# The mixer's first norm factor made on GpSimd instead of TensorE, ScalarE and VectorE

## Chip, core and metric

The kernel runs on one core of one Trainium2 chip. The metric is the device time of one execution in microseconds. Five engines work side by side, each through its own queue in order: TensorE (PE, with its weight loads as PEld), VectorE (DVE), ScalarE (ACT), GpSimd (POOL) and SyncE (SP), which here only issues DMAs. They wait for one another on semaphores.

## The reference

One step of a decoder trunk for 512 new prompt tokens and 8 decode tokens, 1024 features, one layer: a half-step SwiGLU FFN, a hybrid mixer, another half-step FFN, a final norm. What matters is how the mixer's input is normed and where that goes:

```python
def _rms_norm(x, g):
    y = xf * lax.rsqrt(jnp.mean(xf * xf, axis=-1, keepdims=True) + EPS)
    return (y * g.astype(jnp.float32)).astype(x.dtype)
...
def _hybrid_mixer(h, ...):
    proj = h @ w_in
    u_pool, z, xbc, dt_raw = jnp.split(proj, ...)
    ...
    dt = jax.nn.softplus(dt_raw + dt_bias)
...
h = h + 0.5 * _swiglu(_rms_norm(h, ffn1_norm[l]), ...)
m, p, c, s = _hybrid_mixer(_rms_norm(h, mix_norm[l]), ...)
```

The causal convolution over x, B and C, a pooling mixer, the scan over chunks of 128 tokens and a gated norm follow inside the mixer.

## The kernel before

Features lie on the 128 partitions (8 blocks of 128), the 520 tokens along the free axis, in two halves of 260 (HALVES). Every weight and activation is split into a high and a low part; a product is three matmuls (high by high, high by low, low by high). ScalarE makes the high part of a weight (whi, thi), VectorE the low part (wlo, tlo) from the raw tile, which SyncE's queue loads.

The norm is applied late. While the first FFN ends, prep makes xh_mx and xl_mx (the features times the norm's weight, not yet times the factor) and adds the squares of the 8 feature blocks into acc_mx. The factor is one number per token, 1 / sqrt(mean + epsilon), wanted on every partition: the tile r_mx, 128 x 520. rstds makes it half by half: a matmul of acc_mx with a matrix of ones sums over the partitions and leaves the sum on all of them (psr_mx, in PSUM), ScalarE takes the root with scale 1/1024 and epsilon as bias, VectorE the reciprocal. in_proj's products (inbc, inx, inp, inz) are made from xh_mx and xl_mx without the factor, and each is multiplied by r_mx when VectorE copies it from PSUM (evac; dv for the step sizes).

The mixer starts with the small product for the step sizes (dt, two halves, in two PSUM banks), then the factor, then dv, then the plan CONV_PLAN, "b0 b1 d0 b2 b3 x0 x1 v0 d1 x2 x3 d2 ...". A b or x is one block of in_proj (inbc00 and inbc01 are the halves of block b0) with its convolution: U is the copy scaled by the factor, A takes one ScalarE pass and three VectorE passes over it, then a Silu. d0 is token_dt: TensorE brings dv into token order (psdv), and a chain of some 20 small steps on VectorE and ScalarE makes the step sizes (dt_v, dt_e, dt_s, dt_q, tok) and dta. d1 is token_acs: TensorE multiplies dta with a triangle (psacs). The mixer has 8 PSUM banks, handed out in turn, so a product that isn't copied out holds its bank.

The order within each engine's queue isn't the order of the code: a list scheduler places the instructions when the program is built, by the dependences, the order of the code as priority, and its own idea of durations. A few are tied by hand (issue_after, keep_in_program_order). GpSimd does small things here: it clears and fills the edges of U, copies states out, and later adds the pooling windows. Its queue holds no DMA between the first FFN's end and the output projection.

Of the kernel before, what the change touches and what calls it, by code (L numbers as in the profile page):

```python
# [4 lines left out]

# [4 lines left out]

F32 = mybir.dt.float32
F32R = mybir.dt.float32r
AF = mybir.ActivationFunctionType
ALU = mybir.AluOpType
# [3 lines left out]
P = 128  # L18
D = 1024
SEQ = 512  # L20
NS = 8
NT = SEQ + NS
HB = NT // 2
HALVES = (slice(0, HB), slice(HB, NT))
# [3 lines left out]
EPS = 1e-6  # L28
# [40 lines left out]
def tile_trunk_step(ctx: ExitStack, tc: tile.TileContext, ins: dict, outs: dict):  # L69
# [733 lines left out]

    ps[0] = tc.alloc_tile_pool(name="ppm", bufs=8, space=PSUM, reuse_waits="tile")
    mixer(tc, ins, outs, dict(locals()))
    f2["xg"].release()
    xa[0].release()
# [90 lines left out]
def mixer(tc, ins, outs, e):  # L898
    nc = tc.nc
    cst, act, wp, tmp, dr, pool = (e[x] for x in ("cst", "act", "wp", "tmp", "dr", "pool"))  # L900
    ones, queued, squared = e["ones"], e["queued"], tuple(e["added"])
    bank, load_unit, mm3, mm_low_last, ws, v, rstd, rstds, vec, h, nx2, raw_tile, open_f2, fin, fill = (
        e[x] for x in ("bank", "load_unit", "mm3", "mm_low_last", "ws", "v", "rstd", "rstds", "vec", "h", "nx2", "raw_tile",
                       "open_f2", "fin", "fill"))
    xh, xl, _, r = nx2[0]
    xa = e["xa"][0]
    mp = pool("mx", "right")
# [45 lines left out]
    for b, hs in enumerate(HALVES):  # L953
        for k in range(KD):
# [2 lines left out]
            nc.tensor.matmul(dtb[b][:48, :HB], w48[:, k], xh[:, k, hs], start=k == 0, stop=k == KD - 1)  # L957
            if not k:
                nc.tensor.matmul(dtb[b][:NH, :HB], w48[:, k, :NH], xl[:, k, hs], start=False, stop=False)
    rstds(nx2[0], "mx")  # L960
    dv = mp.tile([48, NT], F32, tag="h0", bufs=4, name="dv")
    for b, hs in enumerate(HALVES):
        nc.vector.tensor_tensor(out=dv[:, hs], in0=dtb[b][:48, :HB], in1=r[:48, hs], op=ALU.mult)
# [522 lines left out]
```

## Time and profile before

| | |
|---|---|
| time of the kernel, median of 3 runs | 954.13 us (953.25 to 955.27) |
| the profiled execution's own time, first to last instruction (span) | 951.9 us |
| between the span and the median of the runs | 2.2 us |
| TensorE busy | 942.5 us (99%) |
| VectorE busy | 852.7 us (90%) |
| ScalarE busy | 635.7 us (67%) |
| GpSimd busy | 148.3 us (16%) |

The profile is of one execution. A row of the timeline has the start in the span, the duration, the engine, the line of the kernel, the operation with its output and inputs, and in square brackets the idle time before it with what ended it. A group by line or tile gives least, median and longest duration in ns. Starts of successive rows overlap a little, so what an instruction costs its engine is read from start to start.

### The profile page before, as it was taken

How to read it: one execution, taken by the hardware profiler on the slowest of the kernel's cores; microseconds unless marked ns; L12 is line 12 of the kernel's file. 1: busy time of each engine (PE TensorE's matmuls, PEld its weight loads, DVE VectorE, ACT ScalarE, POOL GpSimd, SP SyncE). 2: the span in 40 equal slices, each digit the busy share in tenths (PEclk: the TensorE clock that was granted, in tenths of full speed). 3: DMA queues.
4: the chain of work that ended last, by engine and by line, in shares of the span. 5: the costliest groups of instructions: out<-in, count | busy, mean ns of one | idle time of the engine just before them, and what ended most of it. 6: DMA issues, size and time to landing. Idle time of an engine off the chain costs nothing.

```text
span 951.9 us, 19681 instructions
## 1 busy us (share of the span) xinstructions
PE 942.5 (99%) x7674; PEld 925.9 (97%) x7674; DVE 852.7 (90%) x1462; ACT 635.7 (67%) x1179; POOL 148.3 (16%) x230
## 2 busy tenths in 40 slices
PE   9999999999999999999999999999999999999996
PEld 8999999999999999999999999999999999999996
DVE  6899899998988688789998998999999999999886
ACT  7777756677566455485668735777776676766774
POOL 0011100100100000046251100111112101122120
PEclk9999999999999999999999999999999999999998
DMA  7666554455553343354264453556666655776552
GB/s 205 187 166 150 143 151 135 115 140 156 134 155 95 86 134 122 92 180 138 91 184 133 141 114 115 138 122 160 163 173 176 163 146 144 171 194 185 145 180 91
DMA packets 53995, 138.35 MB, mean 145 GB/s; under 512 B 7750, under 2 KB 15878, under 8 KB 53902
## 3 DMA queue, kind: packets, MB, share of 16 engines
q1 hardware_dynamic: 39918, 104.19, 34.2%
q0 software_dynamic: 13712, 32.78, 18.7%
q8 instruction: 60, 0.98, 0.4%
q14 instruction: 33, 0.27, 0.1%
q10 hardware_dynamic: 272, 0.13, 0.0%
HBM read 129.74 MB, written 7.34 MB: 144 GB/s over the span
## 4 chain that ended last, share of the span: by engine, by line
PE 44%; DVE 2%; issue 1%; POOL 1%; DMA 1%; ACT 1%; DVEq 0%; ACTq 0%; POOLq 0%
PE A L160 8%; PE BE L160 6%; PE wo L160 5%; PE A L165 4%; PE BE L165 3%; PE wo L165 2%; PE P L311 1%; PE dh L155 1%; PE dh L151 1%; PE dh L154 1%; POOL zs L1068 1%; PE inz L151 1%; PE inz L154 1%; PE inz L155 1%; DMA room<-in_state_ssm 1%
## 5 line engine op out<-in xcount | busy, mean ns | idle before, releaser
L504 ACT COPY ac<-A 128x260 f32<-128x260 f32 x85 | 31.6, 372 | 35.4 <-PE A L155 17.3
L433 DVE TENSOR_TENSOR s<-raw 128x1024 f32<-128x1024 f32 x39 | 47.6, 1222 | 4.4 <-DMA raw<-in_w2gu 2.8
L504 ACT COPY ac<-BE 128x260 f32<-128x260 f32 x41 | 15.4, 376 | 33.6 <-PE BE L165 17.7
L151 PE MATMUL inx<-xh_mx,whi_inx 128*128 128x260 f32 x112 | 31.8, 284 | 0.0
L154 PE MATMUL inx<-xl_mx,whi_inx 128*128 128x260 f32 x112 | 31.6, 282 | 0.0
L155 PE MATMUL inx<-xh_mx,wlo_inx 128*128 128x260 f32 x112 | 31.6, 282 | 0.0
L1027 DVE SCALAR_TENSOR_TENSOR A<-U,h,A 128x544 f32<-128x544 f32 x36 | 29.0, 807 | 1.6 <-ACT A L1025 1.2
L311 PE MATMUL P<-x,raw 128*128 128x260 f32 x128 | 28.9, 385 | 0.2 <-DMA raw<-in_w1gu 0.2
L311 PEld LDWEIGHTS P<-x,raw 128*128 128x128 f32 x128 | 24.4, 192 | 4.2 <-DMA raw<-in_w1gu 0.6
L160 PE MATMUL wo<-catg,whi_wo 128*128 128x260 f32 x192 | 27.4, 285 | 0.0
L1193 ACT ACTIVATE so<-br,sxdt 128x128 f32<-128x128 f32 x64 | 22.8, 376 | 5.8 <-DVE room L1195 5.2
L160 PEld LDWEIGHTS wo<-catg,whi_wo 128*128 128x128 f32 x192 | 24.8, 188 | 0.2
L139 ACT CAST thi<-raw 128x1024 fp32r<-128x1024 f32 (+1 forms) x14 | 14.2, 1012 | 15.7 <-PE wo L160 4.8
L1304 DVE TENSOR_TENSOR h<-wo,h 128x260 f32<-128x260 f32 x48 | 19.2, 422 | 5.0 <-PE wo L165 4.7
L252 DVE TENSOR_TENSOR gs<-gq,gs 128x780 fp32r<-128x780 f32 (+1 forms) x28 | 23.3, 831 | 0.0
L151 PE MATMUL inz<-xh_mx,whi_inz 128*128 128x260 f32 x80 | 23.0, 287 | 0.0
L154 PE MATMUL inz<-xl_mx,whi_inz 128*128 128x260 f32 x80 | 22.7, 284 | 0.0
L155 PE MATMUL inz<-xh_mx,wlo_inz 128*128 128x260 f32 x80 | 22.6, 283 | 0.0
L251 ACT CAST gs<-gq 128x780 fp32r<-128x780 f32 (+1 forms) x28 | 20.6, 735 | 1.2 <-DVE gq L555 0.8
L151 PEld LDWEIGHTS inx<-xh_mx,whi_inx 128*128 128x128 f32 x112 | 21.1, 188 | 0.2 <-issue 0.2
L160 PE MATMUL A<-xth_f,qs 128*128 128x260 f32 x84 | 21.2, 283 | 0.0
L160 PE MATMUL A<-xtl_f,qs 128*128 128x260 f32 x84 | 21.2, 284 | 0.0
(3140 smaller groups left out, 4382.9 us busy)
## 6 DMA issues: line engine op xcount, KB each, us to landing
raw<-in_w2gu SPq DMA_DIRECT2D x44, 512.0 KB, 4.4
raw<-in_w1gu SPq DMA_DIRECT2D x41, 512.0 KB, 4.3
raw<-in_w_in SPq DMA_DIRECT2D x24, 512.0 KB, 3.7
raw<-in_w1d SPq DMA_DIRECT2D x16, 512.0 KB, 4.6
raw<-in_w2d SPq DMA_DIRECT2D x16, 512.0 KB, 4.6
raw<-in_w_out SPq DMA_DIRECT2D x12, 512.0 KB, 3.5
ab<-scr_acs SPq DMA_DIRECT2D x8, 512.0 KB, 5.5
h<-in_state_ssm SPq DMA_DIRECT2D x16, 256.0 KB, 3.7
```

The lines of the kernel that those rows point to most:

```text
L151: first = nc.tensor.matmul(ps, whi, xhi, start=start, stop=False, **kw)
L154: nc.tensor.matmul(ps, whi, xlo, start=False, stop=False, **kw)
L155: nc.tensor.matmul(ps, wlo, xhi, start=False, stop=stop, **kw)
L160: mm = nc.tensor.matmul(ps, w, x, start=start, stop=False, **kw)
L165: nc.tensor.matmul(ps, w, xhi[k], start=False, stop=k == len(wlo) - 1, **kw)
L251: cast = nc.scalar.copy(hi, s)
L252: low = nc.vector.tensor_tensor(out=lo, in0=s, in1=hi.bitcast(F32), op=ALU.subtract)
L311: mm = nc.tensor.matmul(self.banks[f, u][b][:, :HB], ws(self.raw[f][:, u], j + 4 * q), xg[:, slot[q]], start=j == q == 0, stop=j == 3 and ...
L433: nc.vector.tensor_tensor(out=s1, in0=diag, in1=up0, op=ALU.add)
L504: self.copied = nc.scalar.copy(keep, out[:, :HB]).ins
L1027: nc.vector.scalar_tensor_tensor(out=A[:, :n], in0=U[:, j : j + n], scalar=w(j), in1=A[:, :n], op0=ALU.mult, op1=ALU.add)
L1193: nc.scalar.activation(out=o[:, q], in_=br, func=AF.Copy, scale=sxdt[:, j, b : b + 1]))
```

## The change

The call of rstds for the mixer is replaced. GpSimd sums acc_mx over the partitions and leaves the sum on all of them (total), multiplies by 1/1024 and adds epsilon, and raises each half to the power of minus one half, from a one-column tile that holds -0.5 and is read again for each column. The result is r_mx as before.

```diff
-from concourse import mybir
+from concourse import bass_isa, mybir
...
-    rstds(nx2[0], "mx")
+    total = mp.tile([P, NT], F32, tag="h0", bufs=4, name="total")
+    power = mp.tile([P, 1], F32, tag="power", name="power")
+    nc.gpsimd.memset(power, -0.5)
+    nc.gpsimd.partition_all_reduce(total, nx2[0][2], P, bass_isa.ReduceOp.add)
+    nc.gpsimd.tensor_scalar(out=total, in0=total, scalar1=1.0 / D, scalar2=EPS, op0=ALU.mult, op1=ALU.add)
+    for hs in HALVES:
+        nc.gpsimd.tensor_tensor(out=r[:, hs], in0=total[:, hs], in1=power.to_broadcast([P, HB]), op=ALU.pow)
     dv = mp.tile([48, NT], F32, tag="h0", bufs=4, name="dv")
```

The scheduler places the mixer's beginning anew. GpSimd's queue before, from the end of the first FFN (U_4431 is the edge-padded copy of block b0, ncp and sconv are states):

```order
L949 MEMSET whi_w_4311 128x384
L1018 MEMSET U_4431 128x3
L1020 COPY U_4431<-sconv 128x8x3
L1032 COPY ncp<-U_4431 128x3
L1033 COPY sconv<-U_4431 128x24
L1018 MEMSET U_4501 128x3
```

And now at the same place (lines move by 6, numbers by one; an ISA row without a tile is a change of GpSimd's library, to the one with the sum and back):

```order
L949 MEMSET whi_w_4311 128x384
L1024 MEMSET U_4430 128x3
L962 MEMSET power 128x1
L963 ISA
L963 ISA total<-acc_mx 128x520
L1026 COPY U_4430<-sconv 128x8x3
L964 ISA
L964 TENSOR_SCALAR total<-total 128x520
L966 TENSOR_TENSOR r_mx<-total,power 128x260 x2
L1038 COPY ncp<-U_4430 128x3
```

Two library changes, the sum, the mean and both powers stand in one row, with one small copy between. The first change waits for nothing; the sum waits for the last addition into acc_mx.

TensorE before, at the end of block b1 (inbc_4452 is its second half):

```order
L155 MATMUL inbc_4452<-xh_mx,wlo_inbc_4448 128x260
L974 MATMUL psdv<-sel,dv 128x16 x4
L974 MATMUL psdv<-sel,dv 8x16
L151 MATMUL inbc_4554<-xh_mx,whi_inbc_4550 128x260
L154 MATMUL inbc_4554<-xl_mx,whi_inbc_4550 128x260
```

TensorE now, at the same place:

```order
L155 MATMUL inbc_4451<-xh_mx,wlo_inbc_4447 128x260
L980 MATMUL psdv<-sel,dv 128x16 x2
L151 MATMUL inbc_4553<-xh_mx,whi_inbc_4549 128x260
L154 MATMUL inbc_4553<-xl_mx,whi_inbc_4549 128x260
L155 MATMUL inbc_4553<-xh_mx,wlo_inbc_4550 128x260
```

psdv's first two chunks, which need the first half of dv, stay behind block b1. The other three now stand three half products later, behind inbc_4621 (the first half of block b3). psacs stays between blocks x1 and x2.

VectorE before, around dta (U_4742 and U_4672 are the copies of blocks x0 and b3):

```order
L941 TENSOR_TENSOR U_4672<-inbc_4623,r_mx 128x8
L992 SCALAR_TENSOR_TENSOR dt_e<-dt_e,dt_s 128x80
L141 TENSOR_TENSOR tlo<-raw,thi 128x1024
L993 SCALAR_TENSOR_TENSOR tok<-dt_v,dt_e 128x80
L1027 SCALAR_TENSOR_TENSOR A_4673<-U_4672,h,A_4673 128x544
L995 TENSOR_TENSOR dta<-tok,am 128x64
L939 TENSOR_TENSOR U_4742<-inx_4692,r_mx 128x260
```

VectorE now, around dta (U_4811 is the copy of block x1, A_4812 its convolution, inx_4762 its second half product):

```order
L940 TENSOR_TENSOR U_4811<-inx_4762,r_mx 128x252
L941 TENSOR_TENSOR U_4811<-inx_4762,r_mx 128x8
L997 SCALAR_TENSOR_TENSOR dt_e<-dt_e,dt_q 128x80
L1033 SCALAR_TENSOR_TENSOR A_4742<-U_4741,h,A_4742 128x544
L141 TENSOR_TENSOR wlo_inp_4984<-raw,whi_inp_4983 128x1024
L997 SCALAR_TENSOR_TENSOR dt_e<-dt_e,dt_q 128x80
L1033 SCALAR_TENSOR_TENSOR A_4812<-U_4811,h,A_4812 128x544
```

Two rows further down the same queue, from the last of the three passes of A_4812 on:

```order
L1033 SCALAR_TENSOR_TENSOR A_4812<-U_4811,h,A_4812 128x544
L997 SCALAR_TENSOR_TENSOR dt_e<-dt_e,dt_q 128x80
L998 SCALAR_TENSOR_TENSOR dt_e<-dt_e,dt_s 128x80
L999 SCALAR_TENSOR_TENSOR tok<-dt_v,dt_e 128x80
L1001 TENSOR_TENSOR dta<-tok,am 128x64
L939 TENSOR_TENSOR U_4891<-inx_4841,r_mx 128x260
```

dta has moved from ahead of the copy of block x0 to behind the last pass over block x1, and the steps of its chain now alternate with convolutions. Ahead of the first dv, where the two reciprocals stood, VectorE has the low halves of three more weights and of the pooling weight (wlo_inbc_4550, tlo, wpo, wlo_inx_4688), and wlo_inx_4758 stands between the two halves of dv.

## Prediction

> **What bounds the kernel now.** I read the page's first part, then the windows around the changed step, then the order in time on TensorE, ScalarE, VectorE and GpSimd there. The page gives busy time, share of the span and instructions.
>
> ```profile
> span 951.9 us, 19681 instructions
> PE 942.5 (99%) x7674; PEld 925.9 (97%) x7674; DVE 852.7 (90%) x1462; ACT 635.7 (67%) x1179; POOL 148.3 (16%) x230
> ```
>
> TensorE is the bound: 9.4 us of its span are idle. The windows show whether that holds at the mixer's start. Columns: stretch, its length, busy time of PE, PEld, DVE, ACT, POOL, then the granted clock.
>
> ```profile
> 355.00:360.00 5.00, 5.00 (x41) 4.74 (x40) 4.89 (x6) 2.99 (x4) 0.21 (x1) 1.00 0.62 187
> 360.00:365.00 5.00, 5.00 (x45) 5.00 (x44) 4.38 (x8) 2.65 (x4) 1.01 (x4) 1.00 0.19 60
> 365.00:370.00 5.00, 5.00 (x43) 4.80 (x42) 3.77 (x10) 3.20 (x5) 0.54 (x4) 1.00 0.62 207
> ```
>
> TensorE never stops there, VectorE is nearly full, GpSimd nearly empty. So a wait put on TensorE here lengthens the kernel one for one, and work taken off VectorE is worth nothing by itself. How the factor is made today (start, duration, engine, line, operation):
>
> ```profile
> 355.05 0.42 DVE L194 TENSOR_TENSOR acc_mx<-acc_mx,sq_mx 128x260 f32<-128x260 f32 x1
> 355.50 0.60 PE L210 MATMUL psr_mx<-acc_mx,ones 128*128 128x260 f32 x2
> 356.73 0.28 PE L154 MATMUL inbc<-xl_mx,thi 128*128 128x260 f32 x1
> 356.85 0.28 PE L155 MATMUL inbc<-xh_mx,tlo 128*128 128x260 f32 x1
> 359.49 1.77 DVE L214 RECIPROCAL r_mx<-r_mx 128x260 f32<-128x260 f32 x1
> 361.79 0.41 DVE L963 TENSOR_TENSOR dv<-dt,r_mx 48x260 f32<-48x260 f32 x1
> 368.18 1.20 PE L974 MATMUL psdv<-sel,dv 48*128 48x16 f32 x10
> 369.30 0.39 PE L151 MATMUL inbc<-xh_mx,whi_inbc 128*128 128x260 f32 x1
> 384.12 0.22 DVE L995 TENSOR_TENSOR dta<-tok,am 128x64 f32<-128x64 f32 x1
> ```
>
> The squares are complete at 355.5, the factor at 361.3. TensorE fills the 5.8 us between with products that need no factor. It first needs it at 368.2 (psdv), and the product that needs the step sizes (psacs, the end of the chain through dta) comes at 392.2:
>
> ```profile
> L1000 PEld LDWEIGHTS psacs<-dta,tri x2: 188/188/188, 392.2 to 392.3; 128*128 128x128 f32 x2
> ```
>
> So the old path is early by 7 us at psdv and by 8 us at psacs.
>
> **The change part by part.** *What goes.* TensorE loses the two sums. From the first of them (355.50) to the second product of in_proj (356.73) are 1.23 us, and three products lie inside, at 0.12 (356.73 to 356.85): the sums cost 0.87 us of TensorE. That is all the change can give directly; TensorE would then reach psdv at 368.18 - 0.87 = 367.3. VectorE loses two reciprocals of 1.77 us, ScalarE two roots and a table load; neither is the bound.
>
> *What comes, on GpSimd.* The nearest rows:
>
> ```profile
> 351.11 0.10 POOL L1018 MEMSET U<- 128x3 f32 x1 [7.22 <-PE dn L155]
> 357.60 0.21 POOL L1020 COPY U<-sconv 128x24 f32<-128x24 f32 x1 [6.39 <-DMA sconv<-in_state_conv]
> 411.05 1.27 POOL L1068 TENSOR_TENSOR PW<-PU 128x654 f32<-128x654 f32 x1
> L1068 POOLq MODIFY_POOL_CONFIG  x2: 11/11/11, 410.9 to 411.0; - x2
> raw<-in_w2gu SPq DMA_DIRECT2D x44, 512.0 KB, 4.4
> ```
>
> One pass over 654 columns takes 1.27 us, so by columns an estimated 1.01 us over 520 and 0.505 us over 260. No row shows a sum over partitions. Its lower end is a tree, 7 passes for 128 partitions, 7.1 us; its upper end one pass for each partition, 127 passes, 128 us. I take 20 passes, 20.2 us: 7 to bring the sum together, 7 to hand it to every partition, and half as much for what doesn't overlap. That is nearer to the tree, since the result must be on all partitions and a single pass is the only priced row.
>
> No row shows a power either. Its lower end is what VectorE's reciprocal costs over a plain instruction of its shape (1.77 over 0.42, 4.2 times): 2.1 us a half. For the rest I count a logarithm, a product and an exponential as elementary passes: 30 of them, 15.15 us a half, twice that at the upper end. 30 is a choice, not a row.
>
> The two changes of GpSimd's library lie between the row above, 0.01 us for a change to the library already there, and a transfer of 512 KB, 4.4 us; I take 4.4, since other code has to come from somewhere. The first is behind a memset that starts at 351.1 and waits for nothing, so it is over by 355.6 and hidden in the wait for the squares; if that cover fails it costs 4.4. The Trainium skill, GPSIMD Engine Reference, section 2.1, gives about 6 us to the first call of freshly loaded code; no run here shows it. By that page the first change ends 1.7 us late and the second takes 1.6 us more, and the forecast would be 3.3 us higher.
>
> Mean and epsilon are one pass, 1.0 us, and a copy of 0.2 us stands between. From the squares to the whole factor: 20.2 + 0.2 + 4.4 + 1.0 + 2 x 15.15 = 56.1 us. The first half is there at 355.5 + 40.9 = 396.4, the second at 411.6.
>
> *VectorE beside it.* The trace shows that the two engines share a way to the memory:
>
> ```profile
> 411.33 2.07 DVE L141 TENSOR_TENSOR wlo_inx<-raw,whi_inx 128x1024 fp32r<-128x1024 f32 x1 [0.41 <-ACT whi_inx L139]
> L141 DVE TENSOR_TENSOR tlo<-raw,thi 128x1024 fp32r<-128x1024 f32 x12 | 14.8, 1235 | 2.2 <-ACT thi L139 2.2
> 362.99 0.69 DVE L1046 TENSOR_TENSOR wpo<-raw,wph 128x512 fp32r<-128x512 f32 x1
> ```
>
> This subtraction takes 1.24 us, but 2.07 when a GpSimd instruction runs from 411.05 to 412.32: it stood 0.8 us until that one ended. In the new order the low halves for the next weights (three of 1.13 and one of 0.69, 4.1 us) stand ahead of the first use of the factor. During the long sum they may be held off, but the library change after it is 4.4 us long and covers them; without that cover they cost up to 4.1 us. One more low half stands between the two uses (1.13 us), and I count it behind the second power.
>
> *Where the lateness meets the end.* The order quoted above shows psdv cut in two and dta moved behind the third pass of A_4812, the convolution of the last product before psacs. Spacing from before (start to start: low half 1.13, pass of A 0.70, half of a product scaled 0.34, its last 8 columns 0.07, small step 0.15, reciprocal 0.56):
>
> ```profile
> 376.75 1.22 DVE L141 TENSOR_TENSOR wlo_inx<-raw,whi_inx 128x1024 fp32r<-128x1024 f32 x1
> 377.88 0.23 DVE L991 SCALAR_TENSOR_TENSOR dt_e<-dt_e,dt_q 128x80 f32<-128x80 f32 x1
> 378.03 0.78 DVE L1027 SCALAR_TENSOR_TENSOR A<-U,h,A 128x544 f32<-128x544 f32 x1
> 378.73 0.42 DVE L939 TENSOR_TENSOR U<-inbc,r_mx 128x260 f32<-128x260 f32 x1
> 379.07 0.23 DVE L991 SCALAR_TENSOR_TENSOR dt_e<-dt_e,dt_q 128x80 f32<-128x80 f32 x1
> 372.75 0.65 DVE L986 RECIPROCAL dt_s<-dt_s 128x80 f32<-128x80 f32 x1
> 373.31 0.37 DVE L939 TENSOR_TENSOR U<-inbc,r_mx 128x260 f32<-128x260 f32 x1
> 381.42 0.16 DVE L941 TENSOR_TENSOR U<-inbc,r_mx 128x8 f32<-128x8 f32 x1
> 381.49 0.23 DVE L992 SCALAR_TENSOR_TENSOR dt_e<-dt_e,dt_s 128x80 f32<-128x80 f32 x1
> ```
>
> TensorE waits at psdv from 367.3 to 396.9 (0.5 us for dv), does the first part (4 of the 10 matmuls that took 1.12 from 368.18 to 369.30, 0.45) and three half products (24 x 0.119 = 2.86 us each) to 405.9, and waits for the second part. VectorE, from 411.6: low half 1.13, dv 0.34, the rest of U_4430 0.41, U_4500 0.75; psdv's second part is read by 414.5. Then, to dta: 18 passes of A (12.6), four products scaled (4 x 0.75 = 3.0), three low halves (3.4), the reciprocal (0.56) and 15 small steps (2.25), 21.8 us in all: 436.3, that is 24.7 us after the factor. TensorE needs five half products from 413.9, is at psacs at 428.2, and waits 8.1 us more. psacs moves from 392.2 to 436.3: 44.1 us late. Later the order of TensorE is as before and TensorE is again the bound, so nothing gives this back. Span 951.9 + 44.1, and the 2.2 us by which the median of the runs, 954.1, lies over that span: 998.2 us. In general the delay is the chain's length less 12.0 us.
>
> There is a floor: dta stands behind rows that need the last product before psacs. With a chain of no length TensorE ends that product at 392.2 - 0.87 = 391.3, and then 0.2, the rest of U_4811 0.41, four passes of A 2.8, a low half 1.13 and eight small steps 1.2 remain: psacs at 397.0, 4.8 us late. The floor decides below a chain of 16.8 us.
>
> The clock is left at 0 in the sum, though the trace shows it falling when TensorE is idle (same columns, at the end):
>
> ```profile
> 946.00:948.00 2.00, 0.00 (x0) 0.00 (x0) 1.96 (x4) 0.00 (x0) 0.00 (x0) 0.76 0.50 170
> 948.00:950.00 2.00, 0.00 (x0) 0.00 (x0) 0.00 (x0) 0.00 (x0) 0.00 (x0) 0.50 1.02 351
> ```
>
> The first two waits are followed by 8.1 us of slack at psacs, which hides slow products; after the last wait a half product at half speed would cost 2.9 us.
>
> **The rivals.** *Short chain:* tree-like sum and a cheap power, 7.1 + 0.2 + 0 + 1.0 + 4.2 = 12.5 us. Then the floor alone is left: 958.9; up to a chain of 25 us, 967.1. For it: the rows of 0.1 and 0.2 us above show how little of a GpSimd instruction is fixed cost, so 1.01 us a pass may be too much. Against: five instructions, two of them functions. Chance 0.19.
>
> *The sum goes partition by partition:* 127 passes, 128.3 us, chain 164.2, 1106.3 us; the case begins where the chain passes 85 us, 1027. For it: no row shows GpSimd combining partitions at all, and its instructions act on all 128 in the same pass. Against: nothing in this trace. Chance 0.28. The Trainium skill, GPSIMD Engine Reference, section 3.2, gives 247.7 us for a reduction over the partitions of 128 x 2048, by columns an estimated 62.9 us here: by that page the chain is 98.8 us and the time 1040.9. It speaks against this change; no run here shows it.
>
> *Not slower:* the waits are paid back. The place is psacs: if VectorE is through to dta when TensorE ends inx_4762, nothing is lost, and the 0.87 us remain: 953.3. It decides below a chain of 10 us, and the 5.5 us of rows between inx_4762 and dta must be hidden too, by relief of 3.5 us on VectorE and of waits that the modelled ends of TensorE conceal. For it: 8 us of room at psacs today. Against: those rows read that product, so they can't go earlier. Chance 0.03.
>
> **How the numbers follow.** Forecast (chain 25 to 85 us, 967 to 1027): 0.50, likeliest 998.2. For the range, low end: 7 passes and powers of 10 passes, 18.4 us of chain, 6.4 late, 960.5. High end: 50 passes and powers of 60, 116.7 us, 104.7 late, and 4.1 for VectorE held off, 1062.9. About 1 in 10 lies outside on each side. A difference under 0.2% (1.9 us) can't be told from none. Only the last rival is not slower: faster 0.01, same 0.02, slower 0.97.
>
> **What would show it right or wrong.** In the profile after: TensorE idle at psdv's first part for some 30 us, again before its second part by about half a power, and at psacs for 8; the sum some 20 us, each power some 15 us by the starts of GpSimd's instructions. Wrong in size if the sum takes 7 or 63 us. Wrong in kind if TensorE does not wait at psacs though the factor is late, or if the waits add up to the delay and the end does not move by it.

## The result, and the profile after

The changed kernel takes 1044.68 us (median of 4 runs, 1042.65 to 1046.0) against 954.1 us for the kernel before on the same chip (953.25 to 955.27): 1.094 times as long, 95% interval 1.0925 to 1.096. It is 90.6 us slower where the forecast said 44.1. The sign was right, and the time lies inside the stated range (960.5 to 1062.9). The size was off by a factor of two, and the time lies outside the band that the forecast thought likeliest (967 to 1027).

The first part of the page of the changed kernel (busy time, share of the span, instructions):

```profile
span 1043.2 us, 19679 instructions
PE 951.4 (91%) x7670; PEld 933.0 (89%) x7670; DVE 850.1 (81%) x1460; ACT 633.0 (61%) x1175; POOL 246.4 (24%) x235
```

TensorE has 92 us of idle time where it had 9.4. The chain that ended last, in order of time, around the factor (start, length, what):

```profile
354.87 0.42 DVE acc_mx L194
355.29 1.15 DVE wlo_inbc L141
356.44 1.06 issue
357.50 3.29 POOL total L963
361.03 8.04 issue
369.07 0.95 POOL total L964
370.10 83.68 POOL r_mx L966 x2
453.80 0.43 DVE dv L969
```

The squares are complete at 355.3 and the factor at 453.8: 98.5 us of chain, 83.7 of them in the two powers. "Issue" is time in which GpSimd waited for nothing that the profile shows. What stands there is seen in the rows of GpSimd's own queue, grouped by line (two at the sum's line, two at the mean's):

```profile
L963 POOLq MODIFY_POOL_CONFIG  x2: 11/11/11, 351.3 to 351.3; - x2
L964 POOLq MODIFY_POOL_CONFIG  x2: 48/48/48, 360.9 to 361.0; - x2
```

These are the library changes: issued at 351.3 with the sum starting at 357.5, and issued at 361.0 with the mean starting at 369.07. Lines from the list of waits (us in total, times, the longest):

```profile
PE psdv L980 <- DVE dv L969: 74.9, 2, 45.2
DVE dv L969 <- POOL r_mx L966: 72.3, 2, 42.5
PE psacs L1006 <- DVE dta L1001: 6.1, 1, 6.1
```

TensorE waits where the prediction had it wait, but 45.2, 29.7 (the rest of 74.9) and 6.1 us rather than 30, 7 and 8. The end of the path, in order of time, with psah, a small matmul that stands behind psacs in TensorE's queue:

```profile
477.66 0.22 DVE L1001 TENSOR_TENSOR dta<-tok,am 128x64 f32<-128x64 f32 x1
L1006 PE MATMUL psacs<-dta,tri x2: 422/449/476, 477.9 to 478.2; 128*128 128x64 f32 x2
L1016 PE MATMUL psah<-ident,tok x1: 273/273/273, 492.4 to 492.4; 128*64 128x128 f32 x1
```

Before, psacs ran at 392.3 and psah at 404.3:

```profile
L1010 PE MATMUL psah<-ident,tok x1: 273/273/273, 404.3 to 404.3; 128*64 128x128 f32 x1
```

So psacs is 85.6 us late and psah 88.1. The 2.5 us between are the clock. The windows behind psacs (length, busy time of PE, PEld, DVE, ACT, POOL, then the granted clock, the busy share of the DMA engines, GB/s):

```profile
478.00:480.00 2.00, 2.00 (x9) 1.86 (x10) 0.00 (x0) 0.26 (x2) 0.00 (x0) 0.50 0.01 0
480.00:482.00 2.00, 2.00 (x11) 2.00 (x11) 0.00 (x0) 0.00 (x0) 0.00 (x0) 0.50 0.01 1
482.00:484.00 2.00, 2.00 (x13) 2.00 (x12) 0.01 (x1) 0.00 (x0) 0.00 (x0) 0.64 0.11 7
484.00:486.00 2.00, 2.00 (x19) 2.00 (x18) 0.41 (x1) 0.00 (x0) 0.00 (x0) 1.00 0.11 7
```

TensorE is busy again, but at half of its clock for four microseconds and at 0.64 for two more.

### The profile page after: what moved, and what is told of

The parts are those of the page before. It is cut to its first block, busy times and chain, and to the rows that moved or that the text cites. A ratio compares the mean times of both kernels' runs of the same rounds, so it can differ in the third digit from the quotient of the medians.

```text
span 1043.2 us, 19679 instructions
## 1 busy us (share of the span) xinstructions
PE 951.4 (91%) x7670; PEld 933.0 (89%) x7670; DVE 850.1 (81%) x1460; ACT 633.0 (61%) x1175; POOL 246.4 (24%) x235
## 4 chain that ended last, share of the span: by engine, by line
PE 80%; POOL 8%; DVE 6%; issue 2%; DMA 2%; ACT 1%; DVEq 0%; ACTq 0%; POOLq 0%
POOL r_mx L966 8%; PE A L160 7%; PE BE L160 5%; PE P L311 4%; PE A L151 4%; PE wo L160 4%; PE A L155 4%; PE A L154 4%; PE A L165 3%; PE BE L151 3%; PE BE L154 3%; PE BE L155 3%; PE BE L165 3%; PE wo L165 2%; PE inx L151 2%
## 5 line engine op out<-in xcount | busy, mean ns | idle before, releaser
L966 POOL TENSOR_TENSOR r_mx<-total,power 128x260 f32<-128x260 f32 x2 | 83.7, 41840 | 0.1
L980 PE MATMUL psdv<-sel,dv 48*128 48x16 f32 (+1 forms) x10 | 2.2, 338 | 74.9 <-DVE dv L969 74.9
L139 ACT CAST whi_inx<-raw 128x1024 fp32r<-128x1024 f32 x7 | 7.3, 1047 | 57.3 <-PE inbc L154 56.5
L1031 ACT ACTIVATE A<-U,h 128x544 f32<-128x544 f32 x12 | 9.9, 836 | 32.1 <-DVE U L941 32.0
```

The lines of the kernel that those rows point to most:

```text
L966: nc.gpsimd.tensor_tensor(out=r[:, hs], in0=total[:, hs], in1=power.to_broadcast([P, HB]), op=ALU.pow)
```

## The experiments

Theory P: the power is the price, 161 ns for each of 520 columns, and the rest of the chain matters only through the lateness that it adds. Rivals: the library changes make the price (L); the power costs by the call and not by the columns (F); and, for the later runs, VectorE held off by GpSimd's sum makes what is left (V). Behind each time stands its ratio to the kernel before, with the 95% interval in brackets.

### The power replaced by a product

```diff
-        nc.gpsimd.tensor_tensor(out=r[:, hs], ..., in1=power.to_broadcast([P, HB]), op=ALU.pow)
+        nc.gpsimd.tensor_tensor(out=r[:, hs], ..., in1=power.to_broadcast([P, HB]), op=ALU.mult)
```

> The changed kernel with a multiplication in the place of the power, same operands and shapes; the root is left out, so the factors are other numbers. Theory P (the power itself costs 161 ns a column, the rest of GpSimd's chain is 14.9 us): the two rows take about 0.5 us each, the factor is whole 15.9 us after the squares, at 371.1; TensorE waits about 4.4 us at psdv and not at psacs, since dta stands earlier in this build; psacs 3.5 us late, 957.6 us. Rival L (GpSimd's rows are rough, and the 83.7 us put down to the powers hold the tail of the sum and of the library change): the wait stays, over 1000 us. Rival F (a fixed price of some 42 us for an instruction on freshly loaded code): also over 1000 us.

Measured: 962.58 us, 1.0084 [1.0069, 1.0099]. In order of time on GpSimd, and the only wait of TensorE in this stage:

```profile
358.21 3.30 POOL L963 PARTITION_ALL_REDUCE total<-acc_mx  x1 [6.49 <-issue]
369.16 0.61 POOL L964 TENSOR_SCALAR total<-total 128x520 f32<-128x520 f32 x1 [7.49 <-issue]
369.86 1.20 POOL L966 TENSOR_TENSOR r_mx<-total,power 128x260 f32<-128x260 f32 x2
PE psdv L980 <- DVE dv L969: 3.1, 1, 3.1
```

The same two instructions of the same shape take 1.20 us instead of 83.67. Without the power all but 8 us of the slowdown is gone; both library changes are still there, so L falls. The scheduler has also placed psdv (in one piece) and dta (ready before psacs needs it) anew in this build, so the power's share is not read from this run alone: the next three keep the order of the changed kernel. P gave 957.6 us; the measured time is 5 us longer. Two windows show why (columns as above):

```profile
370.00:375.00 5.00, 3.96 (x20) 3.77 (x21) 4.49 (x10) 1.78 (x2) 4.06 (x6) 0.65 0.16 37
375.00:380.00 5.00, 5.00 (x31) 5.00 (x30) 4.12 (x10) 3.65 (x8) 2.63 (x5) 0.67 0.61 218
```

The granted clock is 0.65 and 0.67 in the mean of these windows. In steps of 1 us it is 1.00 up to 371, then 0.50 from 372 to 378, and 1.00 again from 379: a wait of 3.1 us is followed by some 6.8 us at half of the clock, which cost 3.4 us more. Together that is 6.5 us, of which TensorE saves 0.87 by its two sums; psacs was 6.0 us later than before (398.3 for 392.3), in an execution whose mixer began 0.5 us later. That execution's span is 8.8 us longer than before; the last 2.8 us lie behind psacs, where TensorE waits no more than before, in stretches that differ by as much between one run and another (the numbers are below, under "The rest").

### Half of the columns, half of the partitions

```diff
+        for n, op in ((0, ALU.pow), (1, ALU.mult)):
+            cs = slice(hs.start + n * (HB // 2), hs.start + (n + 1) * (HB // 2))
+            nc.gpsimd.tensor_tensor(out=r[:, cs], ..., in1=power.to_broadcast([P, HB // 2]), op=op)
```

> The changed kernel with the power over the first 130 columns of each half and a multiplication over the other 130; the root is left out for those. The order of all engines is that of the changed kernel. Theory P (161 ns a column): powers of 20.9 us, chain 57.4 us, psacs some 44.5 us late, and with the 5.4 us that the changed kernel lost behind psacs 1004 us. Rival F (a fixed price for each power instruction): powers of 41.8 us still, 1045 us. By the predicted walk (delay = chain less 12.0 us) 999.5 us.

Measured: 1003.15 us, 1.0507 [1.0489, 1.0524]. In order of time on GpSimd, the waits of TensorE, and psacs:

```profile
369.68 43.84 POOL L968 TENSOR_TENSOR r_mx<-total,power 128x130 f32<-128x130 f32 x4
PE psdv L982 <- DVE dv L971: 33.1, 2, 24.2
PE psacs L1008 <- DVE dta L1003: 5.5, 1, 5.5
L1008 PE MATMUL psacs<-dta,tri x2: 421/446/472, 437.6 to 437.8; 128*128 128x64 f32 x2
```

Half of the columns cost about half (43.84 us, with two short products among the four rows, for 83.67): F falls. This kernel is also a test of the forecast's walk, since its chain is, by accident, nearly the forecast's (355.5 to 413.5, 58.0 us, against 56.1): psacs at 437.6, forecast 436.3.

The other half-size run keeps all columns and gives the power only partitions 0 to 63:

```diff
+        for n, op in ((0, ALU.pow), (1, ALU.mult)):
+            ps = slice(n * 64, n * 64 + 64)
+            nc.gpsimd.tensor_tensor(out=r[ps, hs], ..., in1=power[ps].to_broadcast([64, HB]), op=op)
```

> The changed kernel with the power on partitions 0 to 63 and a multiplication on 64 to 127, all 520 columns each; the factor of the upper half of the partitions is left out. Theory C (the power costs by columns, 161 ns each, whatever the partitions): two powers of 41.8 us and two products of about 1 us on the path: about 1046. Rival E (it costs by elements): two powers of 21 us, as with half of the columns: about 1004.

Measured: 1045.91 us, 1.0963 [1.0944, 1.0982].

```profile
368.81 85.98 POOL L968 TENSOR_TENSOR r_mx<-total,power 64x260 f32<-64x260 f32 x4
```

Half of the partitions save nothing. The price goes by columns, as in theory C.

### The power without the sum on GpSimd

TensorE sums the squares as before, ScalarE adds mean and epsilon, and GpSimd makes only the power; no library change stands ahead of it.

```diff
-    nc.gpsimd.partition_all_reduce(total, nx2[0][2], P, bass_isa.ReduceOp.add)
-    nc.gpsimd.tensor_scalar(out=total, in0=total, scalar1=1.0 / D, scalar2=EPS, ...)
+    nc.tensor.matmul(sums, ones, nx2[0][2][:, hs], start=True, stop=True)
+    nc.scalar.activation(out=total[:, hs], in_=sums, func=AF.Identity, bias=e["eps"], scale=1.0 / D)
```

> The sum over the partitions back on TensorE, ScalarE copies it out with mean and epsilon, only the power is on GpSimd. Nothing is left out. Theory P: the first power starts at about 356.8 instead of 370.1, each still takes 41.8 us, psacs some 72.5 us late, 1032 us. Theory L (the sum and the library changes make most of the loss): no library but the resident one is needed and no sum is there, so 960 us or less.

Measured: 1028.36 us, 1.0778 [1.0756, 1.0799]. In order of time on GpSimd, and psacs:

```profile
356.23 41.85 POOL L967 TENSOR_TENSOR r_mx<-total,power 128x260 f32<-128x260 f32 x1 [5.51 <-DVE wlo_inbc L141]
398.21 41.80 POOL L967 TENSOR_TENSOR r_mx<-total,power 128x260 f32<-128x260 f32 x1
L1007 PE MATMUL psacs<-dta,tri x2: 422/450/477, 464.7 to 465.0; 128*128 128x64 f32 x2
```

The power alone makes 1028: 74 of the 90 us with no sum, mean or library change on GpSimd. The chain is 355.5 to 440.0, 84.5 us, and psacs is 72.4 us late.

### The sum without the power

GpSimd only sums; root and reciprocal go back to ScalarE and VectorE.

```diff
     nc.gpsimd.partition_all_reduce(total, nx2[0][2], P, bass_isa.ReduceOp.add)
-    nc.gpsimd.tensor_scalar(out=total, in0=total, scalar1=1.0 / D, scalar2=EPS, ...)
-        nc.gpsimd.tensor_tensor(out=r[:, hs], ..., op=ALU.pow)
+        nc.scalar.activation(out=r[:, hs], in_=total[:, hs], func=AF.Sqrt, bias=e["eps"], scale=1.0 / D)
+        nc.vector.reciprocal(out=r[:, hs], in_=r[:, hs])
```

> Nothing is left out: GpSimd sums the squares over the partitions, ScalarE takes the root of the mean plus epsilon and VectorE the reciprocal, as in the kernel before. GpSimd has no mean and no power after the sum, so no second library change stands on the path. Theory P (the power is the price, the rest costs only what it is late at TensorE): sum ready at about 361.8 (squares 355.2, 3.3 of library change left, 3.3 of sum), root with its table load 1.7, two reciprocals of 1.77 in a row: factor at about 366.5 against 367.3, at which psdv wants it; no wait, TensorE saves its 0.87: 953.3. Rival V (the sum holds VectorE off for 2 to 3 us and the low parts come late): a few waits of TensorE on VectorE, 955 to 959, as the kernel with a multiplication came to 962.6 with one library change more on its path.

Measured: 964.32 us, 1.0106 [1.0089, 1.0123]. Neither theory had this. The factor was in time and psacs even early; the time went elsewhere. By tile and in order of time: psacs, the row of GpSimd's queue at the pooling's line, the pooling, the next of VectorE, the longest wait of TensorE (pm is the pooling's product), and yd, products of the scan behind it (for which the kernel before stands below it):

```profile
L1004 PE MATMUL psacs<-dta,tri x2: 218/246/274, 391.7 to 391.8; 128*128 128x64 f32 x2
L1072 POOLq MODIFY_POOL_CONFIG  x2: 11/11/11, 410.4 to 410.4; - x2
423.76 1.27 POOL L1072 TENSOR_TENSOR PW<-PU 128x654 f32<-128x654 f32 x1 [13.38 <-issue]
425.06 0.92 DVE L1083 SCALAR_TENSOR_TENSOR PW<-PW,PU 128x511 f32<-128x511 f32 x2 [12.83 <-POOL PW L1072]
PE pm L151 <- ACT catp L1086: 6.4, 1, 6.4
L1266 PE MATMUL yd<-ab,xdt x128: 272/273/324, 440.1 to 543.9; 128*64 128x128 f32 x128
L1262 PE MATMUL yd<-ab,xdt x128: 272/273/323, 430.4 to 534.9; 128*64 128x128 f32 x128
```

The second library change had not gone. GpSimd's small copies and memsets ran between the sum and the pooling without a change, but the pooling's first operation on two tensors, issued at 410.4, needs the first library back. In the kernel before, the same row at the pooling's line cost nothing (410.9, pooling at 411.05); here the pooling starts after 13.4 us of idle time, 12.7 us later than before. VectorE stands behind it for 12.8 us and TensorE for 6.4 us; after that TensorE's granted clock is 0.50 from 430 to 435, and yd is 9.7 us late. In the changed kernel the same change lay at the mean, inside the chain.

A variant issued an all-reduce of one column from an earlier line, so that the library would be in place before the squares:

```diff
+    early = mp.tile([P, 1], F32, tag="early", name="early")
+    nc.gpsimd.partition_all_reduce(early, ones[:, :1], P, bass_isa.ReduceOp.add)
```

> As the kernel with the root on ScalarE, with an all-reduce of one column at the mixer's start, so that GpSimd's library for the sum is in place before the squares are. Nothing is left out. If the library change is what makes the sum late: the sum begins with the squares at 355.5, ends at 358.8, factor at about 363.5, 4 us early at psdv, 953.3 and no waits. If the sum's hold on VectorE is what costs (rival V): as slow as the kernel without the early one. If library changes cost nothing on the path, both kernels agree within 0.2%.

Measured: 962.6 us, 1.0083 [1.0068, 1.0098]. It does not answer its question: on GpSimd the early sum came to stand straight ahead of the real one. It does bear on the first change. The early sum needs no squares, and yet it starts 6.5 us after its library change was issued (351.3), where the real sums of the other runs start 6.1 to 6.3 us after theirs. That speaks for the change, and not the wait for the squares, as what held the first sum; since the trace names a product of TensorE as what released the early one, it isn't strictly shown.

```profile
357.83 0.40 POOL L925 PARTITION_ALL_REDUCE early<-ones  x1 [6.73 <-PE dt L959]
358.15 4.34 POOL L963 PARTITION_ALL_REDUCE total<-acc_mx  x1
421.89 1.27 POOL L1074 TENSOR_TENSOR PW<-PU 128x654 f32<-128x654 f32 x1 [11.13 <-issue]
```

The same wait stands at the pooling, here 11.1 us. The real sum took 4.34 us here, 1 us longer than in the other runs; why stays open.

### The library brought back early

One GpSimd operation of one column behind the sum, otherwise as the kernel with the root on ScalarE:

```diff
+    back = mp.tile([P, 1], F32, tag="back", name="back")
+    nc.gpsimd.tensor_scalar(out=back, in0=total[:, :1], scalar1=1.0 / D, scalar2=EPS, ...)
```

> As the kernel with the root on ScalarE, with one GpSimd operation of one column right behind the sum. Nothing is left out. Theory B (each sum over the partitions costs GpSimd two library changes, one before it and one before its next arithmetic, and the second costs what waits for it): the change back lies at 361 to 369, where GpSimd has only small copies to make, so the pooling of 411 runs at once; psah 0.7 us earlier than before, and the time 953.5 to 954.5, no measurable difference from before. Rival V (the sum's hold on VectorE, or the later factor, is what cost the kernel with the root on ScalarE its 10 us): about 964 again.

Measured: 955.4 us, 1.0001 [0.9992, 1.001]. In order of time on GpSimd, and yd:

```profile
361.34 0.28 POOL L1026 COPY U<-sconv 128x24 f32<-128x24 f32 x1
368.57 0.18 POOL L963 TENSOR_SCALAR back<-total 128x1 f32<-128x1 f32 x1 [6.95 <-DVE U L941]
411.14 1.28 POOL L1074 TENSOR_TENSOR PW<-PU 128x654 f32<-128x654 f32 x1
L1268 PE MATMUL yd<-ab,xdt x128: 272/273/323, 430.6 to 534.8; 128*64 128x128 f32 x128
```

One instruction of 0.18 us takes away 9 us. The idle time before it is put down to VectorE in the bracket, but it reads nothing of VectorE's, only the sum of 358.16 to 361.45; it stands where the change back stands in the changed kernel and is about as long (6.95 us; 7.0 to 8.1 in the four runs with a mean); behind it wait only copies. Theory B holds and V falls: the sum with its two library changes costs nothing measurable if both lie where nothing waits. It wins nothing measurable either, though TensorE has its two sums less.

## Why the prediction was wrong in size and right in place

**The power: the step that failed.** "30 passes, 15.15 us a half" measured 41.84, 161 ns a column (83.67 / 520), where a pass of the nearest row costs 1.9 ns. The upper end given, 30.3, was also too low, so the bound was no bound. Twice 26.7 us is 53.4 us too little. In the forecast's own measure a half took 83 elementary passes (41.84 / 0.505), not 30. The base, a plain instruction's pass, was the wrong one: nothing in the record ties a power's price to a small multiple of that. Why a power costs so much, no run shows.

**The sum: too high.** "20 passes, 20.2 us" measured 3.29, below the lower end of 7.1. This gave back 16.9 us, and thereby hid a third of the power's error. The rival "partition by partition" (0.28) falls with it, though the time landed where that rival had it (chain over 85 us, over 1027 us): the power took it there. Its estimate from the Trainium skill, GPSIMD Engine Reference, section 3.2, 62.9 us for the sum and 1040.9 for the kernel, came close to the measured time for a wrong reason; the row says 3.29.

**The library changes: one hidden, 4.4 each.** Neither held. The first was to be over by 355.6; it lasted 6.2 us (351.3 to 357.5), and the sum began 2.2 us after the squares. The second took 8.04 us. The Trainium skill, GPSIMD Engine Reference, section 2.1, has about 6 us for the first call of freshly loaded code: this trace agrees for the first change and is above it for the second. It was nearer than the 4.4 of a 512-KB transfer that I took. Together the two cost 5.8 us more than the forecast.

The sum over the chain closes: 56.1 + 53.4 - 16.9 + 2.2 + 3.6 is 98.4, and 98.5 was measured.

**The walk from factor to psacs: right.** "The delay is the chain's length less 12.0 us" gives for three chains that keep the order of the changed kernel's rows around psdv and dta (58.0, 84.5 and 98.3 us, from 355.5; the runs with half of the columns, with the power alone, and the changed kernel) 46.0, 72.5 and 86.3 us at psacs; measured 45.3, 72.4 and 85.6. dta came 24.1 us behind the whole factor; the forecast had 24.7. With the measured chain the forecast's own formula would have given 998.2 + 42.2 = 1040.4.

**The rest, 4.3 us to the measured time, was set to nothing.** The clock after the last wait was left out with "2.9 if not hidden", and it was not: 2.5 us. The wait at psacs is 6.1 instead of 8.1 for the same reason: the products ahead of it were slow as well (granted clock 0.86 in the mean from 454 to 478). About 1.2 us more appear up to the output projection and 2.0 in the second FFN. Its first products (P) and the first of its last stage (dh), in the kernels before and after:

```profile
L311 PE MATMUL P<-xg_f,raw x64: 380/382/383, 584.9 to 613.8; 128*128 128x260 f32 x64
L151 PE MATMUL dh<-g,dhi_2d x48: 278/282/287, 914.5 to 942.0; 128*128 128x260 f32 x48
L311 PE MATMUL P<-xg_f,raw x64: 380/382/383, 674.2 to 703.1; 128*128 128x260 f32 x64
L151 PE MATMUL dh<-g,dhi_2d x48: 278/282/288, 1005.8 to 1033.3; 128*128 128x260 f32 x48
```

From P to dh are 329.6 us before and 331.6 after. No instruction there has changed, and the run with half of the partitions has the same P (674.2) and ends 1.7 us earlier. Over all nine traces this stretch takes 329.3 to 331.6 us, and the one from psah to P, in the seven that do not wait at the pooling, 180.4 to 181.8 (before: 180.6). The shortest of both, 329.3 and 180.4, are in the run with the power alone, where TensorE comes 72 us late; so the 1.2 and the 2.0 us are differences between one execution and another, as far as these traces tell. The three pieces make 5.7 us; the formula is 0.7 too long at psacs (86.3 for 85.6), and the median lies 1.5 us over the profiled span instead of 2.2, which leaves 4.3.

**VectorE held off: wrong as to the power, right as to the sum.** The low half that was counted behind the second power (1.13 us) ran beside it in its usual time; the one beside the sum did stand until the sum ended. In order of time on VectorE:

```profile
358.03 2.82 DVE L141 TENSOR_TENSOR wlo_inbc<-raw,whi_inbc 128x1024 fp32r<-128x1024 f32 x1 [1.60 <-ACT whi_inbc L139]
422.74 1.23 DVE L141 TENSOR_TENSOR wlo_inx<-raw,whi_inx 128x1024 fp32r<-128x1024 f32 x1 [9.98 <-ACT whi_inx L139]
```

**Short chain and its floor: not tested.** Wherever the power was taken away, the rows around dta were put in another order; in the kernel with a product dta is ready at 389.9, where the floor has psacs at 397.0. **Not slower** needed a chain under 10 us; with the power it cannot be had.

**What was not seen:** where the change back belongs. The prediction had it and priced it, between the sum and the mean, and the expectation of the first run without power and mean had no second change on the path. It belongs to the sum: it has its price wherever the next instruction of the other library stands, and without the mean that is the pooling.

## What to carry to other kernels

An instruction whose price no row shows cannot be bounded by multiples of the cheapest row: where nothing else is to be had, let the upper end be several times wider, or ask what the forecast would be if that one term were three times as large, since this decides the size here. On GpSimd count the functions that need another library, put a change in front and a change behind, and look for the place where each would be hidden; a dummy instruction of one column moved the one behind and was worth 9 us. And after a wait on TensorE add the slow products that follow: 3.1 us of waiting cost about 6 here, and 6.4 us at the pooling about 10.

## What the runs showed of the hardware

- A power on GpSimd takes 161 ns a column at 128 partitions and as much at 64; a product of the same shape 0.6 us for 260 columns, 2.3 ns a column: about 70 times less.
- A sum of 128 x 520 over the partitions, result on all of them, takes 3.29 to 3.30 us in six runs, and 4.34 us in the one where a sum of one column stands straight ahead of it.
- From the issue of a library change to the instruction behind it pass 6.1 to 6.5 us ahead of the sum, 7.0 to 8.0 us behind it, and 11.1 and 13.4 us at the pooling. In its first 10 us at the pooling the DMA engines were busy, as the windows of the kernel with the root on ScalarE show (next to last column 0.86 and 0.79). But that does not explain it: over the whole stretch there the DMA share is 0.68 for 13.4 us, at the pooling of the run with the early sum 0.81 for 11.1 us, and at the first change of the changed kernel 0.66 for 6.2 us. The cause stays open.

```profile
410.00:415.00 5.00, 5.00 (x45) 5.00 (x45) 1.82 (x6) 2.65 (x5) 0.20 (x1) 1.00 0.86 246
415.00:420.00 5.00, 5.00 (x44) 5.00 (x44) 0.00 (x0) 1.48 (x3) 0.00 (x0) 1.00 0.79 282
```
